# The last 512 columns of v by seven block products, with the mixes' sums by transfer

## The chip, the cores and the metric

The kernel runs on one core of a Trainium2 chip. The time is the device time of one execution in microseconds; before the change it is 993.88 us, the median of three runs (993.27 to 995.94). The core has five engines that run side by side and meet at semaphores: PE (matrix products, with PEld loading its weights), DVE (element by element), ACT (functions and scaled copies), POOL (here fills and the transfers that add), and SP (here transfers alone). Each works its own list in order.

## The reference

Two layers over 512 positions of 1024 channels. The first is a pooling and convolution mixer, the second gated linear attention; each is followed by a gated convolution network. The change lies in the attention's input projection:

```python
q, k, v, r, gl = jnp.split(h, [GLA_DK, 2 * GLA_DK, 2 * GLA_DK + GLA_DV, 2 * GLA_DK + 2 * GLA_DV], axis=-1)
g = jax.nn.log_sigmoid((gl @ w_g2 + b_g).astype(f32)) / GLA_TAU
...
o = o_intra + jnp.einsum('bhnlk,bhnkv->bhnlv', q_in, states)
```

Here `h` is the normed input times `gla_w_in`; q and k have 512 columns, v and r 1024, gl 16. Head h of four uses v's columns 256h to 256h + 255, so v's last 512 columns belong to heads 2 and 3. Inputs and results are float32.

## The kernel before

All activations lie in SBUF with channels on the 128 partitions and 512 positions along the row, as 8 tiles `x`. To keep float32 accuracy, each operand of a product is split in two parts: a high part, a rounding copy on ACT (`hi`, `xh`, `th`), and a low part, what is left, on DVE (`lo`, `xl`, `tl`). A product then takes three passes on PE: high by high, high by low, low by high.

Most projections use seven block products for eight: operands are halved both ways, sums of the quarters are formed, and seven products p1 to p7 of quarter size give the result (`DOWN_SEVEN` is their order). The weights' sums are made on the way in: SP loads a quarter into `s31` (L487), POOL adds two others to it with an accumulating transfer (L491), DVE forms `s2` (L520) and `s4` (L526), and ACT and DVE split the four pieces a1, s31p, s2 and a2 (L509, L515). The sums of x, the *mixes*, come from `mix_parts` (L401 to L437): `ta` and `tb` of each pair of x tiles hold four half-row sums, made on DVE (L413 to L422) from `xg`, a scaled copy by ACT (L406), and then split (L428, L434). p1, p2 and p3 use x's own parts, p5 and p7 use `ta`, p6 and p4 use `tb`.

The attention stage lies between 462.5 and 612 us. First v and gl come by plain products with positions on the partitions: `v_chunk` (L1313 to L1315) in four blocks, of 272 columns (256 of v and 16 of gl) and three of 256, each over eight tiles of x. `v_out` (L1320) copies each result with the scale `y4n` to `vt`, `v_low` (L1330) forms its low part `vl`. Between the chunks stand the sums of squares `ss` (L365), their root y4 on ACT and DVE (L323 to L331), its spread `bc` (L357), the transposes `glT`, and four products z (L1259), the gates' logits, to which DVE adds the bias (L1261). ACT then takes abs, exp and log of each z (L1265, L1269, L1273). After v come four q/k pairs and four r pairs of seven products (L627), with the heads' scores, states and outputs between them.

`run_plan` sets the order: each step is given a planned time by `at`, the steps are sorted by it, and PE, DVE and ACT get their instructions in just that order. SP and POOL are not in the plan's lists; a scheduler places their transfers. Raw weight blocks have three buffers (`raw`), the weight sums of this stage two (`s31`), PSUM eight banks. ACT loads a table of functions when it changes between a root, exp, log and others.

Of the kernel before, what the change touches and what calls it, by code (L numbers as in the profile page):

```python
# [14 lines left out]
P = 128  # L15
# [8 lines left out]
NTT = T // P  # L24
HEADS = 4
EPS = 1e-6
VG = 1040
RANK = 16
STACK = 96
VG_COLS = (272, 256, 256, 256)  # L30
VG_K = ((3, 3, 2), (4, 4), (4, 4), (4, 4))
WBLK = 1024
WPITCH = WBLK + 64
SKEW = 19
# [8 lines left out]
UNIT = 1.364  # L43
MM = 0.2272
PAIR = 7 * UNIT
PLAIN = 8 * UNIT
NORM = 0.46
PE_AT = {"p1": 0, "p2": 1, "p6": 3, "p5": 5, "p7": 6, "p4": 9, "p3": 11}
# [17 lines left out]
VLOW = (1.6, 1.6, 1.6, 1.6)  # L66
ROWS = (1.6, 0.6, 3.6)
SILU = 5.6
ROOT = 2.2
L31 = (-1.4, -1.4)  # L70
KEYS = 1.6
GATE = 3.0
MIXL = 5.8
HALF_AT = ((11.0, 6.6, 5.6), (13.0, 5.2, 4.3))
LEFT_AT = 2.6
EARLY = (0, 2, 4)
# [16 lines left out]


@with_exitstack
def trunk_kernel(ctx, tc, xT, cols, w_first, w_lead, w_ab, w_pool, w_abo, w_vg, w_qk, w_r, w_g2, w_go, w_up, w_dn, w_ds, w_de, out):
    nc = tc.nc
    V, S, G, PE = nc.vector, nc.scalar, nc.gpsimd, nc.tensor

# [8 lines left out]
    def slot(dt=F32, name="s"):  # L108
        return big.tile([P, T], dt, tag="s", name=name)
# [17 lines left out]
    def bank(name="ps"):  # L127
        return ps.tile([P, T], F32, tag="ps", name=name)
# [8 lines left out]
    def col(name, i=0):  # L137
        c = COLS[name] + i
        return colt[:, c : c + 1]
# [56 lines left out]
    def f32(ap):  # L196
        return ap.bitcast(F32)
# [203 lines left out]
    def mix_parts(i, gname, minus_gain):  # L401
        m = {}

        def scale():
            m["x"] = slot(name="xg")
            S.activation(m["x"], x[i], AF.Copy, scale=col(gname, i))  # L406

        def first_sum():
            if "t" in m:
                return  # L410
            xg = m["x"]
            m["t"] = slot(name="ta"), slot(name="tb")
            V.tensor_tensor(m["t"][0][:, lo_t], xg[:, lo_t], xg[:, hi_t], ALU.subtract)  # L413

        def sums():
            xg, x2 = m["x"], x[i + HK]
            first_sum()
            ta, tb = m["t"]
            gain, minus = col(gname, i + HK), minus_gain[:, i : i + 1]
            V.scalar_tensor_tensor(tb[:, lo_t], x2[:, hi_t], gain, ta[:, lo_t], ALU.mult, ALU.add)  # L420
            V.scalar_tensor_tensor(tb[:, hi_t], x2[:, lo_t], minus, tb[:, lo_t], ALU.mult, ALU.add)
            V.scalar_tensor_tensor(ta[:, hi_t], x2[:, hi_t], gain, xg[:, hi_t], ALU.mult, ALU.subtract)  # L422

        def high():
            m["h"] = {}
            for n in (1, 0):
                m["h"][n] = slot(F32R, "th")
                S.activation(m["h"][n], m["t"][n], AF.Copy)  # L428
# [9 lines left out]
        return scale, first_sum, sums, high, low  # L438

    def operands(mixed):  # L440
# [14 lines left out]
    def at(t, fn):  # L455
        events.append((t, len(events), fn))
# [21 lines left out]
        at(t_high, lambda: steps[0]())  # L478
        at(t_low, lambda: steps[1]())

    def seven_weights(src, base, pool, sums, behind=False, lead=None, later=0.0, begin=(26.0, 20.0, 15.4, 9.7), early=0.0, low31=None):
        w = {}

        def load_sum():
# [16 lines left out]
        def tiles(kind, wide):  # L501
            if wide:
                return wsp.tile([P, WPITCH], F32R, tag=kind, name=kind)[:, SKEW : SKEW + WBLK]
            tag, bufs = "s" + kind[0], 2 if pool == "up" else 1
            return stage[pool].tile([P, T + 64], F32R, tag=tag, name=tag, bufs=bufs)[:, SKEW : SKEW + T]

# [32 lines left out]
        when = (-6.75, -4.35, -2.7, -2.4, -1.65, -0.95, -0.3, 1.55, 1.5, 3.3)  # L539
        if pool == "up":  # L540
            when = (*when[:7], *((2.2, 1.5, 4.4) if lead is not None else (0.4, 1.5, 3.3)))
        if pool == "dn":
            when = (-4.2, -2.9, 0.0, -4.0, -2.2, -1.0, -0.3, 4.3, 0.9, 7.2)
        if pool == "gla":
            when = (-6.75, -4.35, -2.1, -1.6, -0.9, -0.2, 0.5, 4.4, 1.5, 5.3)
        if low31 is not None:
            when = (*when[:8], low31, when[9])
        if lead is not None and lead < 2:
# [708 lines left out]
    def gate_logits(h):  # L1257
        zb = bank("z")
        PE.matmul(zb, g2[:, h * P : (h + 1) * P], glT, start=True, stop=True)  # L1259
        heads[h]["z"] = slot(name="z")  # L1260
        V.tensor_scalar(heads[h]["z"], zb, col("b_g", h), None, ALU.add)  # L1261

    def gate_sizes(h):
        e = heads[h]["e"] = slot(name="e")
# [223 lines left out]
        at(t + 0.8, high)  # L1488
        at(t + split, low)

    def mix_in_plan(i, t, last=4.2):
        scale, _, sums, high, low = mix_parts(i, "mix1", minus_gain)

        def done():
            mixed[i] = low()

        at(t, scale)
        at(t + 0.8, sums)
        at(t + 3.0, high)
        at(t + last, done)  # L1500

    t = 0.0

    def then(us, fn):
        nonlocal t
        at(t, fn)
        t += us
# [6 lines left out]
    minus_gain = negated("mix1", 0.0)  # L1514
    mixed = [None] * HK
    for i in range(HK):
        mix_in_plan(i, (7.0, 11.6, 21.0, 25.6)[i], MIXL if i == 2 else 4.2)
    first = True
    for b, (n, ks) in enumerate(zip(VG_COLS, VG_K)):
        k0 = 0  # L1520
# [30 lines left out]
    def pair(src, kind, h, between=None, early=0.0, begin=(26.0, 20.0, 15.4, 9.7), calm=None, low31=None):  # L1551
# [58 lines left out]
        else:  # L1610
# [4 lines left out]
            at(t + soon, lambda: silu(0, left))  # L1615
            at(t + (SILU if h == 1 else soon + 0.7), lambda: silu(1, right))

    def head_keys(h, d=0.0):
        at(t + d, lambda: keys(h))
        at(t + d + 2.4, lambda: keys2(h))  # L1620

    def head_scores(h):
        then(2.1, lambda: scores(h))
        at(t + 0.1, lambda: key_rows(h))
        at(t + 0.1, lambda: masked(h))
        at(t + ROWS[0], lambda: masked_high(h))
        at(t + ROWS[1], lambda: key_lows(h))
        at(t + ROWS[2], lambda: masked_low(h))

    def head_kv(h):  # L1630
        then(1.3, lambda: kv(h))
        at(t + 0.1, lambda: states(h))
# [8 lines left out]
    def gates_of(h, t):  # L1641
        at(t + 2.0, lambda: decays(h))
        at(t + 1.6, lambda: decays2(h))
        at(t + 5.8, lambda: decays3(h))

    def head_gates(h, d, split):
        for e in range(2):
            out_gate(h, e, t + d + 0.75 * e, split)

    gates_of(0, t - 4.0)  # L1650
    pair(w_qk, "qk", 0, calm=0, low31=L31[0])
    head_keys(0, KEYS)
    gates_of(1, t - GATE)
    at(t - 7.5, lambda: log_gate3(3))
    pair(w_qk, "qk", 1, low31=L31[1])
    head_keys(1, 0.2)
    gates_of(2, t - 3.0)
    head_scores(0)
# [211 lines left out]
```

## Time and profile before

| what | value |
|---|---|
| median of three runs | 993.88 us |
| span of the profiled execution | 992.2 us |
| mean granted clock of PE | 0.998 |
| first product of v's block 0 | 462.5 us |
| first product of block 2, first product of q/k pair 0 | 489.0, 511.0 us |

The page gives the profiled execution by its span, from the first to the last instruction; the median of the timed runs is 1.7 us above it, which is what lies around the span and the spread of runs together. In a timeline row stand the start, the time taken, engine, line, operation, output and inputs, shapes, how many such instructions follow each other, and in brackets the idle time ahead with what ended it. An instruction's time overlaps the next one's a little, so a queue's pace is read from start to start.

### The profile page before, as it was taken

Reading aid. Unit: us, or ns where it says so; the run is one execution under the profiler, and the core shown is the slowest. Engines: PE = TensorE matmul, PEld = TensorE weight load, DVE = VectorE, ACT = ScalarE, POOL = GpSimd, SP = SyncE. Lnnn points to the kernel's source line nnn. Section 1 sums busy time; section 2 is a strip of 40 time slices with the busy share of each in tenths; the row PEclk is TensorE's granted clock in tenths of the full one; section 3 lists DMA queues with packets and bytes.
Section 4 is the critical chain, followed back from the end, with each engine's and each line's share of the span. In section 5 each row is a group of like instructions: output and inputs, shape, how many; then the busy total and the mean of one; then the engine's idle time right before and its main releaser. Section 6 shows DMA issues by size and latency. Waiting matters only on the chain.

```text
span 992.2 us, 18669 instructions
## 1 busy us (share of the span) xinstructions
PE 983.8 (99%) x7356; PEld 932.6 (94%) x7356; DVE 891.8 (90%) x1399; ACT 624.7 (63%) x1040; POOL 89.1 (9%) x111
## 2 busy tenths in 40 slices
PE   9999999999999999999999999999999999999997
PEld 7888889999999988999999999899999999988997
DVE  7786689999999999889999889889999999999886
ACT  6432467666667666446776676667766766666553
POOL 0000111101011000002000000111111101000000
PEclk9999999999999999999999999999999999999999
DMA  7423667778877464726426453767788787464622
GB/s 255 130 98 106 167 141 180 192 184 210 202 185 199 103 166 114 189 82 178 123 82 160 108 132 115 193 160 179 205 213 193 191 208 178 120 146 125 168 81 99
DMA packets 69240, 155.22 MB, mean 156 GB/s; under 512 B 5824, under 2 KB 9280, under 8 KB 69152
## 3 DMA queue, kind: packets, MB, share of 16 engines
q1 hardware_dynamic: 50560, 119.03, 37.6%
q0 software_dynamic: 18304, 34.61, 21.3%
q8 instruction: 57, 0.93, 0.4%
q10 hardware_dynamic: 288, 0.40, 0.1%
q14 instruction: 31, 0.25, 0.1%
HBM read 149.29 MB, written 2.10 MB: 153 GB/s over the span
## 4 chain that ended last, share of the span: by engine, by line
PE 90%; DVE 5%; ACT 2%; issue 1%; DMA 1%; DVEq 0%; ACTq 0%
PE stx L627 31%; PE styz L627 17%; PE dn L287 11%; PE go L287 4%; PE abo L287 4%; PE dn L627 3%; PE stz L627 2%; PE pu L1094 2%; PE pc L287 2%; PE pb L287 2%; PE px L287 2%; PE vg L1313 1%; PE vg L1315 1%; PE vg L1314 1%; DMA raw<-in_w_up 1%
## 5 line engine op out<-in xcount | busy, mean ns | idle before, releaser
L515 DVE TENSOR_TENSOR lo<-raw,hi 128x1024 fp32r<-128x1024 f32 x120 | 146.3, 1221 | 3.2 <-ACT hi L509 2.9
L509 ACT ACTIVATE hi<-raw 128x1024 fp32r<-128x1024 f32 x120 | 125.6, 1058 | 35.6 <-PE styz L627 11.2
L491 POOL DMA_DIRECT2D s<-in_w_up x44 | 53.4, 1213 | 477.9 <-ACT yh L200 96.0
L242 ACT ACTIVATE hi<-raw 128x1024 fp32r<-128x1024 f32 (+3 forms) x67 | 59.8, 896 | 26.8 <-PE px L287 9.0
L384 DVE SCALAR_TENSOR_TENSOR cacc<-u,colt,cacc 128x511 f32<-128x511 f32 x96 | 71.6, 746 | 2.6 <-ACT cacc L381 2.5
L246 DVE TENSOR_TENSOR lo<-raw,hi 128x1024 fp32r<-128x1024 f32 (+3 forms) x67 | 68.6, 1028 | 5.3 <-ACT hi L242 4.6
L515 DVE TENSOR_TENSOR lo<-s,hi 128x1024 fp32r<-128x1024 f32 x60 | 73.1, 1218 | 0.0
L381 ACT ACTIVATE cacc<-u,colt 128x512 f32<-128x512 f32 x48 | 39.2, 816 | 43.6 <-DVE u L749 40.0
L627 PE MATMUL stx<-th,hi 128*128 128x256 f32 x416 | 64.6, 277 | 0.8 <-ACT kk L734 0.8
L509 ACT ACTIVATE hi<-s 128x1024 fp32r<-128x1024 f32 x60 | 63.4, 1056 | 2.8 <-issue 1.6
L627 PE MATMUL stx<-th,lo 128*128 128x256 f32 x416 | 64.1, 276 | 0.0
L627 PE MATMUL stx<-tl,hi 128*128 128x256 f32 x416 | 64.1, 276 | 0.0
L627 PE MATMUL styz<-xh,hi 128*128 128x256 f32 x400 | 62.0, 277 | 0.0
L627 PE MATMUL styz<-xh,lo 128*128 128x256 f32 x400 | 61.8, 276 | 0.0
L627 PE MATMUL styz<-xl,hi 128*128 128x256 f32 x400 | 61.6, 276 | 0.0
L627 PEld LDWEIGHTS stx<-th,hi 128*128 128x128 f32 x416 | 54.9, 188 | 1.3 <-ACT kk L734 1.0
L627 PEld LDWEIGHTS stx<-tl,hi 128*128 128x128 f32 x416 | 54.9, 188 | 0.0
L627 PEld LDWEIGHTS stx<-th,lo 128*128 128x128 f32 x416 | 54.9, 188 | 0.0
L627 PEld LDWEIGHTS styz<-xh,hi 128*128 128x128 f32 x400 | 52.9, 188 | 0.1
L627 PEld LDWEIGHTS styz<-xh,lo 128*128 128x128 f32 x400 | 52.8, 188 | 0.0
L509 ACT ACTIVATE sh<-raw 128x512 fp32r<-128x512 f32 x60 | 37.9, 631 | 23.8 <-DVE raw L520 23.7
L627 PEld LDWEIGHTS styz<-xl,hi 128*128 128x128 f32 x400 | 52.8, 188 | 0.0
(416 smaller groups left out, 2704.5 us busy)
## 6 DMA issues: line engine op xcount, KB each, us to landing
s<-in_w_up SPq DMA_DIRECT2D x44, 512.0 KB, 6.7
s<-in_w_up POOLq DMA_DIRECT2D x44, 512.0 KB, 7.2
raw<-in_w_up SPq DMA_DIRECT2D x44, 512.0 KB, 6.4
raw<-in_w_up SPq DMA_DIRECT2D x44, 256.0 KB, 3.2
raw<-in_w_dn SPq DMA_DIRECT2D x32, 320.0 KB, 2.9
raw<-in_w_ab SPq DMA_DIRECT2D x12, 512.0 KB, 3.7
raw<-in_w_abo SPq DMA_DIRECT2D x8, 512.0 KB, 3.5
s<-in_w_ds SPq DMA_DIRECT2D x8, 512.0 KB, 5.8
```

Source lines behind the costliest of these rows:

```text
L242: S.activation(parts[0], raw, AF.Copy)
L246: V.tensor_tensor(parts[1], raw, f32(parts[0]), ALU.subtract)
L287: PE.matmul(out, w[k] if isinstance(w, list) else w[:, k, :], a[k], start=first and i == 0 and k == 0, stop=last and i == 2 and k == n - 1 ...
L381: S.activation(acc[0], u, AF.Identity, bias=col(bname, j), scale=col(wname, 2 * nj + j))
L384: V.scalar_tensor_tensor(a, u[:, : T - i], col(wname, (2 - i) * nj + j), a, ALU.mult, ALU.add)
L491: G.dma_start(w["s31"].rearrange("p (a n) -> p a n", a=2), part, accum_op=ALU.add)
L509: S.activation(h, src(), AF.Copy)
L515: V.tensor_tensor(lo, src(), f32(h), ALU.subtract)
L627: PE.matmul(b[out][:, ts], wt[k], a[k], start=first and i == 0 and k == 0, stop=i == 2 and k == len(a) - 1, skip_group_check=True,)
L1094: PE.matmul(pus[g], parts[k][w][:, g * P : (g + 1) * P], a[k], start=k == 0 and i == 0, stop=k == KD - 1 and i == 2,)
L1313: PE.matmul(o[c][:, :n], xh[kk][:, cs], h[:, k, :], start=kk == 0, stop=False)
L1314: PE.matmul(o[c][:, :n], xl[kk][:, cs], h[:, k, :], start=False, stop=False)
```

## The change

v's first 512 columns (and gl) stay with `v_chunk`, in two blocks. The last 512 are computed by a new `v_pair`, with seven block products, each in two halves of the channels (n = 0 and 1), so there are two sets of seven-weights, loaded from a new array `w_v`. The products' results are copied out of PSUM by ACT (`keep`) and summed by DVE (`add`) as raw rows `vs`, four tiles of 512. Only in the fourth q/k pair are these scaled and split into `vt` and `vl` (`finish`). Since p6, p5 and p7 of `v_pair` need the mixes, these are made earlier, and another way: ACT writes the x part of `tb`, DVE makes the two sums of `ta`, and two accumulating transfers on POOL add `ta` to `tb` and one half of `tb` to the other. The bias of z moves from DVE to ACT. The weight sums of q/k pairs 0 and 1 are loaded later, since `v_pair` takes the two `s31` buffers first.

```diff
-VG_COLS = (272, 256, 256, 256)
+VG_COLS = (272, 256)
+V_WHEN = (
+    (-7.5, -6.0, 1.0, -0.6, 0.2, 1.0, 1.8, 6.0, 3.2, 8.4),
...
+MIX_AT = ((2.0, 17.0), (4.0, 19.0), (6.0, 21.0), (8.0, 24.0))
...
+    def mix_by_dma(i, gname, minus_gain):
+        def scale():
+            m["x"] = slot(name="xg")
+            S.activation(m["x"], x[i], AF.Copy, scale=col(gname, i))
+        def start():
+            tb = slot(name="tb")
+            m["t"] = [slot(name="ta"), tb]
+            S.activation(tb[:, lo_t], x[i + HK][:, hi_t], AF.Copy, scale=col(gname, i + HK))
+            S.activation(tb[:, hi_t], x[i + HK][:, lo_t], AF.Copy, scale=minus_gain[:, i : i + 1])
+        def sums():
+            xg, (ta, tb) = m["x"], m["t"]
+            V.tensor_tensor(ta[:, lo_t], xg[:, lo_t], xg[:, hi_t], ALU.subtract)
+            V.scalar_tensor_tensor(ta[:, hi_t], x[i + HK][:, hi_t], col(gname, i + HK), xg[:, hi_t], ALU.mult, ALU.subtract)
+        def first_add():
+            G.dma_start(tb[:, lo_t], ta[:, lo_t], accum_op=ALU.add)
+        def second_add():
+            G.dma_start(tb[:, hi_t], tb[:, lo_t], accum_op=ALU.add)
...
         heads[h]["z"] = slot(name="z")
-        V.tensor_scalar(heads[h]["z"], zb, col("b_g", h), None, ALU.add)
+        S.activation(heads[h]["z"], zb, AF.Identity, bias=col("b_g", h))
...
+        for wait, step in zip((0.0, 0.7, 0.8, 0.9, 4.5), steps):
+            at(t + wait, step)
+        for n, when in ((0, t + 2.6), (1, late)):
+            at(when, lambda n=n: high(n))
+            at(when + 0.8, lambda n=n: done(n))
...
+    def v_pair():
+            for n in range(2):
+                h, lo = w[n][piece]
+                for c in range(2):
+                    cs = slice(c * P, (c + 1) * P)
+                    for i, (a, wt) in enumerate(((ah, h), (al, h), (ah, lo))):
+                        for k in range(2):
+                            cols = slice(side * QUARTER + k * 256, side * QUARTER + k * 256 + 256)
+                            PE.matmul(b[out][:, c * 256 : c * 256 + 256], a[2 * n + k][:, cs], wt[:, cols],
...
+        def keep(tile, sign):
+            for c in range(2):
+                S.activation(rows_of(tile, c), b["x"][:, c * 256 : c * 256 + 256], AF.Copy, scale=sign)
...
+        for name in DOWN_SEVEN:
+            then(VUNIT, lambda name=name: product(name))
+            ends_at[name] = t
+        at(ends_at["p1"] + 0.1, lambda: keep((0, 0), 1.0))
+        at(ends_at["p6"] + 0.1, lambda: keep((0, 1), 1.0))
...
+        def finish(now):
+            for c in range(NTT):
+                at(now + 1.8 * c, lambda c=c: scaled(c))
+                at(now + 1.8 * c + 0.8, lambda c=c: lows(c))
...
     head_scores(1)
+    finish_v(t + 1.0)
     pair(w_qk, "qk", 3, {3: (lambda: head_kv(1),)}, 4.6)
```

The first place where the order of instructions moves is ACT's list from the logits to the first results. Before, DVE had added the bias, and ACT had the copies of block 1 (`vt`), the abs (`e<-z`) and the first exps (`e<-e`) there, with the splits of a mix between them:

```order
L1320 ACTIVATE vt<-vg_5576,y4n 128x256
L1320 ACTIVATE vt<-vg_5577,y4n 128x256
L1265 ACTIVATE e<-z 128x512
L1320 ACTIVATE vt<-vg_5578,y4n 128x256
L1265 ACTIVATE e<-z 128x512 x2
L1320 ACTIVATE vt<-vg_5579,y4n 128x256
L1265 ACTIVATE e<-z 128x512
L1269 ACT_TABLE_LOAD
L1269 ACTIVATE e<-e 128x512 x2
L428 ACTIVATE th<-tb 128x512
L428 ACTIVATE th<-ta 128x512
L242 ACTIVATE hi<-raw 128x1024
```

After the change, the same stretch of ACT's list, right behind the splits of the mixes' `tb`, begins with the four biases:

```order
L1308 ACTIVATE z<-z,colt 128x512 x4
L1367 ACTIVATE vt<-vg_5612,y4n 128x256
L554 ACTIVATE hi<-raw 128x512
L1367 ACTIVATE vt<-vg_5613,y4n 128x256
L1312 ACTIVATE e<-z 128x512
L1367 ACTIVATE vt<-vg_5614,y4n 128x256
L554 ACTIVATE hi<-s_5466 128x1024
L1312 ACTIVATE e<-z 128x512 x2
L1367 ACTIVATE vt<-vg_5615,y4n 128x256
L1312 ACTIVATE e<-z 128x512
L1316 ACT_TABLE_LOAD
L1316 ACTIVATE e<-e 128x512 x2
```

The four biases, the split of 512 columns (s2 of the first half) and that of 1024 (its s31p) came in; the row that follows is the two copies of p1's result (`vs<-vx`, 128x256 each), which so stand behind the first two exps.

The second place is ACT's list around the root y4 (`y<-ss`). Before:

```order
L325 ACT_TABLE_LOAD
L325 ACTIVATE y<-ss,eps_t 128x4
L428 ACTIVATE th<-tb 128x512
L428 ACTIVATE th<-ta 128x512
L242 ACTIVATE hi<-raw 128x1024
L406 ACTIVATE xg<-xall,colt 128x512
L1530 ACTIVATE rs<-bc 128x512
```

Before these rows stood one `xg`, of mix 0. After the change, the list ahead of the same root, from the second `xg` on:

```order
L451 ACTIVATE xg<-xall,colt 128x512
L474 ACTIVATE th<-ta 128x512
L456 ACTIVATE tb<-xall,colt 128x256
L457 ACTIVATE tb<-xall,minus_gain 128x256
L248 ACTIVATE hi<-raw 128x1024
L451 ACTIVATE xg<-xall,colt 128x512
L474 ACTIVATE th<-ta 128x512
L456 ACTIVATE tb<-xall,colt 128x256
L457 ACTIVATE tb<-xall,minus_gain 128x256
L451 ACTIVATE xg<-xall,colt 128x512
L474 ACTIVATE th<-ta 128x512
L331 ACT_TABLE_LOAD
```

All four `xg`, three pairs of `tb` halves, three splits of `ta` and one weight split now stand ahead of the table load and the root.

The third place is POOL's list in this stage. After the change (the `tb` rows are the mixes' additions; before, the second fill of `att` was followed at once by the weight sums of q/k pair 2):

```order
L534 DMA s_5466<-in_w_v 128x2x512
L534 DMA s_5535<-in_w_v 128x2x512
L1251 MEMSET starts 128x512
L1255 MEMSET maskf 128x512
L1253 MEMSET starts 128x1 x8
L1261 MEMSET att 128x512
L1257 AFFINE_SELECT maskf<-maskf 128x512
L1261 MEMSET att 128x512
L466 DMA tb<-ta 128x256 x2
L470 DMA tb<-tb 128x256 x2
L466 DMA tb<-ta 128x256
L470 DMA tb<-tb 128x256
```

Eight transfers of 128 KB came in, each `tb<-tb` behind a wait for its `tb<-ta`; first and second additions of mixes 2 and 3 alternate.

More of the change, by code (lines that the diff above doesn't have):

```diff
@@ L45 @@
 PAIR = 7 * UNIT
+VUNIT = 2 * UNIT
 PLAIN = 8 * UNIT
@@ L72 @@
 GATE = 3.0
-MIXL = 5.8
 HALF_AT = ((11.0, 6.6, 5.6), (13.0, 5.2, 4.3))
@@ L438, in mix_parts, with high, low @@
         return scale, first_sum, sums, high, low
+    def mix_by_dma(i, gname, minus_gain):
+        m = {}
+        def scale():
[11 more added lines that the diff above has]
+        def first_add():
+            ta, tb = m["t"]
+            G.dma_start(tb[:, lo_t], ta[:, lo_t], accum_op=ALU.add)
+        def second_add():
+            tb = m["t"][1]
+            G.dma_start(tb[:, hi_t], tb[:, lo_t], accum_op=ALU.add)
+        def high(n):
+            m["h", n] = slot(F32R, "th")
+            S.activation(m["h", n], m["t"][n], AF.Copy)
+        def low(n):
+            lo = slot(F32R, "tl")
+            V.tensor_tensor(lo, m["t"][n], f32(m["h", n]), ALU.subtract)
+            return m["h", n], lo
+        return scale, start, sums, first_add, second_add, high, low
     def operands(mixed):
@@ L479, in block, with seven_weights @@
         at(t_low, lambda: steps[1]())
-    def seven_weights(src, base, pool, sums, behind=False, lead=None, later=0.0, begin=(26.0, 20.0, 15.4, 9.7), early=0.0, low31=None):
+    def seven_weights(src, base, pool, sums, behind=False, lead=None, later=0.0, begin=(26.0, 20.0, 15.4, 9.7), early=0.0, low31=None, when=None, shared=None):
         w = {}
@@ L1489, in out_gate, with mix_in_plan, done @@
         at(t + split, low)
[L1491 to L1500, printed above, removed]
+    def mix_in_plan(i, t, late):
+        *steps, high, low = mix_by_dma(i, "mix1", minus_gain)
+        mixed[i] = {}
+        def done(n):
+            mixed[i][n] = low(n)
+        for wait, step in zip((0.0, 0.7, 0.8, 0.9, 4.5), steps):
[3 more added lines that the diff above has]
+            at(when + 0.8, lambda n=n: done(n))
     t = 0.0
@@ L1654, in trunk_kernel @@
     at(t - 7.5, lambda: log_gate3(3))
-    pair(w_qk, "qk", 1, low31=L31[1])
+    pair(w_qk, "qk", 1, begin=(19.0, 14.5, 15.4, 9.7), low31=L31[1])
     head_keys(1, 0.2)
```

74 lines of the change are left out of this document (66 added, 8 removed).

## The prediction

> **The bound.** I read the page's busy times first, then its chain, then the busy times by stretch around the stage that changes (columns: PE, PEld, DVE, ACT, POOL, clock, DMA share, GB/s), and last the timelines.
>
> ```profile
> PE 983.8 (99%) x7356; PEld 932.6 (94%) x7356; DVE 891.8 (90%) x1399; ACT 624.7 (63%) x1040; POOL 89.1 (9%) x111
> PE 90%; DVE 5%; ACT 2%; issue 1%; DMA 1%; DVEq 0%; ACTq 0%
> 480.00:490.00 10.00, 9.81 (x82) 9.29 (x81) 9.83 (x19) 6.60 (x13) 0.00 (x0) 1.00 0.42 121
> 490.00:500.00 10.00, 10.00 (x91) 10.00 (x90) 8.29 (x16) 9.94 (x17) 0.00 (x0) 1.00 0.19 62
> 500.00:510.00 10.00, 10.00 (x91) 10.00 (x90) 9.90 (x15) 7.18 (x11) 0.00 (x0) 1.00 0.17 57
> ```
>
> PE is the bound: 99% busy, 90% of the chain, and here full at a clock of 1.00. So work taken from PE shortens the run, and any new wait of PE lengthens it by its own length. ACT, 63% over the span, is full in 490 to 500, just where the products of v's last columns now run.
>
> **PE's saving.** The rows are PE's, from its timeline (start, length, line).
>
> ```profile
> 475.44 1.05 PE L357 MATMUL bc<-ident,y 128*128 128x128 f32 x8
> 487.69 1.09 PE L1259 MATMUL z<-glT,g2s 96*128 96x512 f32 x4
> 488.97 0.39 PE L1313 MATMUL vg<-hi,xh 128*128 128x256 f32 x1 [0.19 <-DVE z L1261]
> 510.86 0.33 PE L1549 MATMUL stx<-ones 128*128 128x64 f32 x2
> ```
>
> From 488.97 to 510.86 PE runs 192 products of 256 columns for blocks 2 and 3: 21.89 / 192 = 0.114 us each. The seven products have 7 x 24 = 168. -2.7 us, and the 0.19 us wait for DVE's z goes too: -0.2. The rest of PE's order is unchanged. One of the seven (24 matmuls) takes 2.74 us.
>
> **The root.** PE's bc at 475.44 needs y4, the root of the sums. The rows are ACT's timeline, and one of DVE.
>
> ```profile
> 465.76 0.73 ACT L306 ACTIVATE xh<-xall,colt 128x512 fp32r<-128x512 f32 x1 [4.68 <-DVE xall L910]
> 466.91 1.59 ACT L242 ACTIVATE hi<-raw 128x544 fp32r<-128x544 f32 x2
> 469.13 1.28 ACT L325 ACT_TABLE_LOAD   x1
> 472.73 0.26 ACT L325 ACTIVATE y<-ss,eps_t 128x4 f32<-128x4 f32 x1 [2.31 <-DVE v L323]
> 473.42 0.16 DVE L331 SCALAR_TENSOR_TENSOR y<-t,y 128x4 f32<-128x4 f32 x1
> ...
> 487.70 0.71 ACT L406 ACTIVATE xg<-xall,colt 128x512 f32<-128x512 f32 x1
> 488.31 0.81 ACT L1320 ACTIVATE vt<-vg,y4n 128x256 fp32r<-128x256 f32 x2
> 489.03 0.62 ACT L1265 ACTIVATE e<-z 128x512 f32<-128x512 f32 x1
> 489.55 0.47 ACT L1320 ACTIVATE vt<-vg,y4n 128x256 fp32r<-128x256 f32 x1
> 491.96 1.28 ACT L1269 ACT_TABLE_LOAD   x1
> 493.25 1.16 ACT L1269 ACTIVATE e<-e 128x512 f32<-128x512 f32 x2
> 494.31 0.62 ACT L428 ACTIVATE th<-tb 128x512 fp32r<-128x512 f32 x1
> 495.36 1.04 ACT L242 ACTIVATE hi<-raw 128x1024 fp32r<-128x1024 f32 x1
> 496.30 1.14 ACT L1269 ACTIVATE e<-e 128x512 f32<-128x512 f32 x2
> 498.75 2.20 ACT L1273 ACTIVATE e<-e 128x512 f32<-128x512 f32 x4
> 500.86 1.05 ACT L242 ACTIVATE hi<-raw 128x1024 fp32r<-128x1024 f32 x1
> 512.68 0.39 ACT L1571 ACTIVATE q<-stx 128x256 f32<-128x256 f32 x1 [0.47 <-PE stx L627]
> 512.96 0.63 ACT L1298 ACTIVATE bc<-bc 128x512 f32<-128x512 f32 x1
> ```
>
> From start to start ACT takes: xg 0.61, a half with a column scale (vt) 0.36, 512 columns 0.52, 1024 columns 0.94, a table load 1.29, two exps 1.06, four logarithms 2.11, a plain half 0.28. Before, the table load sat idle from 469.13 and y waited for DVE. Now, between the splits that start at 466.91 and y, stand one of 544 (0.55), 4 xg (2.44), 6 halves tb (2.16), 3 splits th (1.56), one of 1024 (0.94) and the load (1.29): 8.9 us, so y starts at 475.8. y4 is done 0.85 later, as before (472.73 to 473.58): 476.7 against 475.44. +1.3 on PE. The tb halves are not in the trace; between the plain half and vt the term is 0.8 to 1.3, and two waits on DVE in between could make it 1.7.
>
> **The mixes.** Eight accumulating transfers of 128 KB go through POOL's queue, behind the two weight sums and the memsets that end near 470.7.
>
> ```profile
> 464.90 2.46 POOL L491 DMA_DIRECT2D s<-in_w_qk  x2 [48.92 <-DMA s<-in_w_qk]
> s<-in_w_qk POOLq DMA_DIRECT2D x2, 512.0 KB, 9.5
> 648.95 0.90 POOL L674 DMA_DIRECT2D acc<-sq  x1 [8.15 <-DMA acc<-sq]
> 653.97 0.86 POOL L674 DMA_DIRECT2D acc<-sq  x1 [3.22 <-DMA acc<-sq]
> DMA to landing us min/median/max: 3.3/5.3/10.5
> ```
>
> The second weight sum is issued near 466.1 and lands 9.5 or more later, so the first mix transfer, queued behind it, lands near 478. Then POOL, in order and 0.87 us a piece, issues second(0), second(1), first(2) at 479.7, waits L for its landing, second(2), first(3), waits L, second(3), waits L: the last lands at 480.6 + 3L. On ACT its split (0.52) and z of head 0 (0.6) follow, and PE's p1 needs that z, whose bank it takes: 481.8 + 3L, against 488.97 + 1.3 = 490.3. The trace has such transfers of 256 KB only, 3.3 to 10.5 us, and POOL restarted 5.0 us after one issued at 648.95. Half the bytes: I bound L by 1.7 (half the shortest) and 5.3 (the median), and take 3.6, nearest the shortest row with some restart. 492.6: +2.3 (0 to 7.4; the wait begins at L = 2.8). Behind that split ACT holds all four z, and DVE behind its low part the first s2 sum, which p6 needs; both lie beside this wait and the next.
>
> [...]
>
> **The stop at p6.** p6 writes the bank of p1, so it waits until ACT has copied p1 out (vs). In ACT's order between z of head 0 and the second vs stand 3 z, 4 vt (1.44), a half-width split (0.52), 4 abs (2.08), one of 1024 (0.94), a load (1.29), 2 exps (1.06), 2 vs (0.56). Scaled z is not in the trace: 0.52 as e, 0.82 as the row of the convolution below, 0.6 taken as xg: 1.8. In all 9.8 us; PE needs 2 x 2.74 = 5.5 for p1 and p2. +4.3 (4.0 to 5.0).
>
> ```profile
> L381 ACT ACTIVATE cacc<-u,colt 128x512 f32<-128x512 f32 x48 | 39.2, 816 | 43.6 <-DVE u L749 40.0
> 516.03 2.36 DVE L515 TENSOR_TENSOR lo<-raw,hi 128x1024 fp32r<-128x1024 f32 x2
> 499.42 0.69 DVE L1277 SCALAR_TENSOR_TENSOR z<-z,e 128x512 f32<-128x512 f32 x1 [1.64 <-ACT e L1273]
> 500.14 1.22 DVE L1279 TENSOR_TENSOR_SCAN bc<-starts,z 128x512 f32<-128x512 f32 x1
> ```
>
> Then 2 exps (1.06), a half split (0.52), a load (1.29), 4 logarithms (2.11), the second half's s31p split (1.05) and behind it its low part on DVE (1.22): 7.3 us, where PE, from p6, comes there after 2.74 + 1.37 + 0.45 = 4.6. +2.8 (2.2 to 3.2).
>
> DVE follows from there: until the second half's low a2, 2 z (0.72 each), 2 scans (1.14) and 2 lows (1.14, 1.22), 6.0 against PE's 5.4: +0.5. Until sh of pair 0, a scan and its z, 8 adds of halves (0.34), a low and two of 512 (0.6), then on ACT sh, two vs and the copy of p1 (1.5): about 7.7 against PE's 6.4 (p4, p1, p2 and a rest), and 0.5 more at its p7: +1.8. Together +2.3 (1.0 to 3.5).
>
> **Fourth pair.** It gains four lows of 512 on DVE and four copies on ACT.
>
> ```profile
> 540.00:550.00 10.00, 10.00 (x85) 9.84 (x84) 9.93 (x21) 6.77 (x18) 1.20 (x1) 1.00 0.65 153
> 556.00 1.08 DVE L1417 SCALAR_TENSOR_TENSOR st<-st,dec,kv 128x256 f32<-128x256 f32 x2 [1.45 <-ACT st L1415]
> 980.00:992.00 12.00, 6.45 (x56) 6.14 (x54) 6.07 (x14) 2.87 (x6) 0.00 (x0) 0.87 0.49 175
> ```
>
> DVE is full up to 550 and has 1.45 idle at 556; 4 x 0.7 = 2.8. +1.1 (0 to 2.8). ACT has room there.
>
> DVE's relief hides nothing: the sums of the mixes (8 halves), four lows, z and eight vl leave it, but two sets of seven-weight splits come in their place. The weight loads keep their places on SP behind the same buffers; their cover is the same stalls.
>
> **Sum** against the profiled span: -2.7 - 0.2 + 1.3 + 2.3 + 4.3 + 2.8 + 2.3 + 1.1 = +11.2, 992.2 to 1003.4. The median of the runs is 1.7 above that span: 1005.1.
>
> **Rivals.**
> - Mixes in time (L up to 2.8): the third term falls, +8.9, 1002.8. For it: only half the bytes, and few other transfers after 480 (DMA share 0.42, 0.19). Against it: the shortest row is 3.3. Chance 0.22. [...]
> - Mixes late (L = 5.3): +16.3, 1010.2. Chance 0.12.
> - The clock falls in PE's new gap of 4 us at p6: for it, the last 12 us, with PE idle for 5.5, show 0.87. That is 12 x 0.13 = 1.6 more, 1006.7. Against: every stretch with short gaps shows 1.00. Chance 0.06. [...]
> - The other side: ACT's list from z to vs ends within p1 and p2. It decides at 5.5 us for 18 instructions; then the terms at p6, p5 and pair 0 fall, and with the mixes in time -2.9 + 1.3 + 1.1 = -0.5, 993.4. Against: each duration above is from a row, and z cannot start before PE's z. Chance 0.07. With y4 and the fourth pair hidden as well, -2.9: 991.0, chance 0.03.
> - That the change does not do what it says is excluded by PE's order: 168 products for 192.
>
> **Numbers.** The forecast, 1005.1, has 0.50. The range takes in mixes in time with every other term at its low end, 1000, and late mixes, 1010, with some of the high ends: 999.5 to 1012.5. A difference of 0.3% (3 us, 990.9 to 996.9) is what a measurement can tell from none: faster 0.02, same 0.08, slower 0.90.
>
> **What would show it.** PE should stop at bc until ACT's y; at p1 for ACT's z, with POOL waiting for its own transfers; at p6 for ACT's vs; in p5 for ACT's hi and DVE's lo. If PE runs through p1 to p4 without a stop and ACT's list is short, I am wrong; if the stop at p1 is long, only L is off.

## The result, and the profile after

The changed kernel takes 1007.09 us, the median of four runs (1006.71 to 1008.92), against 993.58 us before (four runs, 992.86 to 995.94): slower by a ratio of 1.0137, 95% interval 1.0120 to 1.0153. The prediction was 1005.1 with a range of 999.5 to 1012.5. The profiled execution has a span of 1007.2 us. Of all executions reported below one, the profiled one of the run e10_both, ran at a mean clock of 0.65 and took 1413.33 us; it is left out there.

The page after, busy times and chain:

```profile
PE 988.1 (98%) x7332; PEld 934.6 (93%) x7332; DVE 893.6 (89%) x1399; ACT 634.7 (63%) x1060; POOL 97.7 (10%) x121
PE 89%; DVE 4%; ACT 3%; DMA 2%; issue 1%; POOL 0%; DVEq 0%; POOLq 0%; ACTq 0%
```

PE runs 24 instructions less and is busy for 4.3 us longer, 2.7 of them in the stage measured below (146.35 for 143.69). So beside the waits some of its products became slower: at half clock p1's 24 took 5.18 us, as shown below, where 24 at full clock take 2.80. The stretches of the changed kernel (same columns as in the prediction) say where:

```profile
490.00:500.00 10.00, 5.14 (x26) 4.62 (x25) 3.96 (x6) 4.82 (x10) 0.87 (x1) 0.73 0.10 14
500.00:510.00 10.00, 8.41 (x63) 7.92 (x62) 5.90 (x11) 9.94 (x17) 0.99 (x1) 0.93 0.24 79
510.00:520.00 10.00, 8.28 (x67) 7.67 (x66) 7.76 (x10) 8.11 (x14) 1.42 (x2) 1.00 0.75 186
```

Between 490 and 500 every engine is idle for about half of the time or more, and the clock is below 1: all wait for something that is none of them. PE's waits of the changed kernel from 460 to 650 (who, for whom: total us, times, longest):

```profile
PE vx L1702 <- ACT z L1308: 4.9, 1, 4.9
PE bc L363 <- DVE y L337: 1.6, 1, 1.6
PE vx L1702 <- ACT vs L1716: 1.6, 1, 1.6
PE vz L1702 <- ACT hi L554: 1.1, 1, 1.1
PE stx L674 <- ACT q L1620: 0.9, 2, 0.7
PE kv L1448 <- DVE ktl L1442: 0.6, 1, 0.6
PE vz L1702 <- DVE lo L560: 0.5, 1, 0.5
PE stx L674 <- ACT k L1620: 0.4, 1, 0.4
```

These are the stops that were forecast (bc, p1, p6, the high and the low part that p5 needs for its second half, pair 0, and the heads around the fourth pair). Before, PE had one wait of 0.2 us in the same stretch.

The profiles of this study differ by up to 3.5 us in when this stage begins (470.1 to 473.7), with the same products of PE ahead of it. So I measure the **stage** from the first product `ss` to the first product `go`, in each profile. The rows are PE's timeline, two of before and two of the changed kernel:

```profile
471.55 0.95 PE L365 MATMUL ss<-ones,acc 128*128 128x1 f32 x8
615.49 1.53 PE L287 MATMUL go<-yh,hi 128*128 128x512 f32 x6
```

```profile
472.48 0.95 PE L371 MATMUL ss<-ones,acc 128*128 128x1 f32 x8
630.59 1.53 PE L293 MATMUL go<-yh,hi 128*128 128x512 f32 x6
```

143.94 us before, 158.11 after: the stage lost 14.17 us, and 0.93 of the 15.0 us between the spans was there before it began. By the starts of PE's products, the loss falls into the pieces of the table. A stage is read from one execution of each kernel, while the times of one kernel's runs mostly differ by 0.3 (e9_dve_bias) to 4.4 us (e1_warm). A difference of some tenths between two stages therefore shows nothing alone.

| piece of the stage | forecast | measured |
|---|---|---|
| to `bc` (root) | +1.3 | +1.8 |
| to the first product of p1 (z's old wait of 0.2 gone, mixes) | +2.1 | +4.8 |
| p1 to the start of pair 0 (26.80 for 21.89 us) | +4.4 | +4.9 |
| pair 0 | +2.3 | +1.4 |
| from there to `go` | +1.1 | +1.3 |
| sum | +11.2 | +14.2 |

The late start of p1 is POOL's chain. POOL's timeline of the changed kernel:

```profile
471.49 1.80 POOL L466 DMA_DIRECT2D tb<-ta  x2
479.84 0.90 POOL L470 DMA_DIRECT2D tb<-tb  x1 [6.55 <-DMA tb<-ta]
...
481.65 1.16 POOL L466 DMA_DIRECT2D tb<-ta  x1
486.44 0.86 POOL L470 DMA_DIRECT2D tb<-tb  x1 [3.62 <-ACT th L474]
486.98 1.22 POOL L466 DMA_DIRECT2D tb<-ta  x1
492.41 0.87 POOL L470 DMA_DIRECT2D tb<-tb  x1 [4.21 <-issue]
```

POOL issues a first addition, waits for it, issues the second, and again for mix 3. (The releaser named at 486.44 is a guess of the profile: that transfer waits for the first addition to the same `tb`.) From 481.65 the three waits are 4.8, 5.4 and, to the split on ACT at 495.18, 2.8 us. ACT's timeline from there, and last one row of DVE:

```profile
495.18 0.63 ACT L474 ACTIVATE th<-tb 128x512 fp32r<-128x512 f32 x1 [5.31 <-DMA tb<-tb]
495.71 2.41 ACT L1308 ACTIVATE z<-z,colt 128x512 f32<-128x512 f32 x4
505.49 0.64 ACT L1716 ACTIVATE vs<-vx 128x256 f32<-128x256 f32 x2
511.09 1.04 ACT L554 ACTIVATE hi<-s 128x1024 fp32r<-128x1024 f32 x1
512.17 1.23 DVE L560 TENSOR_TENSOR lo<-s,hi 128x1024 fp32r<-128x1024 f32 x1 [2.37 <-ACT hi L554]
```

ACT does not stop again until the split at 511.09; DVE's low part of it ends at 513.40, and p5 goes on at 513.45. From the start of z to there the list takes 17.7 us. And PE, with the granted clock of the first stretches (columns: length, PE busy, PEclk, DMA share, GB/s):

```profile
496.44 0.80 PE L1702 MATMUL vx<-hi,xh 128*128 128x256 f32 x2 [4.86 <-ACT z L1308]
501.62 0.40 PE L1702 MATMUL vy<-hi,xh 128*128 128x256 f32 x2
506.18 0.50 PE L1702 MATMUL vx<-hi,th 128*128 128x256 f32 x2 [1.59 <-ACT vs L1716]
```

```profile
494.00:495.00 1.00, 0.00 (x0) 0.82 0.75 107
495.00:496.40 1.40, 0.00 (x0) 0.50 0.00 0
500.00:501.00 1.00, 1.00 (x7) 0.50 0.00 0
```

The clock went to half while PE stood still, and p1's 24 products took 5.18 us (496.44 to 501.62) where p7 later takes 2.80.

### The profile page after: what moved, and what is told of

Its sections match the earlier page's. It is cut to its first block, busy times and chain, and to the rows that moved or that the text cites. A ratio compares the mean times of both kernels' runs of the same rounds, so it can differ in the third digit from the quotient of the medians.

```text
span 1007.2 us, 18674 instructions
## 1 busy us (share of the span) xinstructions
PE 988.1 (98%) x7332; PEld 934.6 (93%) x7332; DVE 893.6 (89%) x1399; ACT 634.7 (63%) x1060; POOL 97.7 (10%) x121
## 4 chain that ended last, share of the span: by engine, by line
PE 89%; DVE 4%; ACT 3%; DMA 2%; issue 1%; POOL 0%; DVEq 0%; POOLq 0%; ACTq 0%
PE stx L674 33%; PE styz L674 19%; PE dn L293 10%; PE go L293 4%; PE abo L293 4%; PE dn L674 3%; PE pu L1141 2%; PE stz L674 2%; PE pc L293 2%; PE pb L293 2%; PE px L293 2%; DMA tb<-ta 1%; ACT hi L554 1%; PE stw L674 1%; DMA tb<-tb 1%
## 5 line engine op out<-in xcount | busy, mean ns | idle before, releaser
L560 DVE TENSOR_TENSOR lo<-raw,hi 128x1024 fp32r<-128x1024 f32 (+1 forms) x126 | 152.4, 1211 | 8.3 <-ACT hi L554 7.8
L554 ACT ACTIVATE hi<-raw 128x1024 fp32r<-128x1024 f32 (+1 forms) x126 | 131.0, 1051 | 34.1 <-PE styz L674 11.0
L560 DVE TENSOR_TENSOR lo<-s,hi 128x1024 fp32r<-128x1024 f32 x62 | 75.4, 1217 | 2.4 <-ACT hi L554 2.4
L248 ACT ACTIVATE hi<-raw 128x1024 fp32r<-128x1024 f32 (+3 forms) x63 | 55.7, 885 | 29.1 <-PE px L293 9.1
L252 DVE TENSOR_TENSOR lo<-raw,hi 128x1024 fp32r<-128x1024 f32 (+3 forms) x63 | 63.6, 1014 | 8.1 <-ACT hi L248 7.4
L554 ACT ACTIVATE hi<-s 128x1024 fp32r<-128x1024 f32 x62 | 65.5, 1057 | 2.4 <-issue 1.3
```

What stands on the lines that cost most here:

```text
L248: S.activation(parts[0], raw, AF.Copy)
L252: V.tensor_tensor(parts[1], raw, f32(parts[0]), ALU.subtract)
L554: S.activation(h, src(), AF.Copy)
L560: V.tensor_tensor(lo, src(), f32(h), ALU.subtract)
```

## The experiments

Two theories stood against each other. **A**: from the moment that the last addition is split, ACT's list (with DVE's steps between) runs in order to the second half of p5, and sets the time; what PE does or suffers ahead of that, slow clock included, costs nothing. **B**: PE's stop at p1 and the slow clock behind it are lost as such, and each microsecond of them is one of the run. All changes are to the changed kernel or to the experiment named.

**PE kept busy through its stop.**

```diff
         zb = bank("z")
+        for _ in range(20 if h == 3 else 0):
+            PE.matmul(zb, g2[:, h * P : (h + 1) * P], glT, start=True, stop=True)
```

> Only change to the changed kernel: 20 more z products of head 3 (96x512, about 0.22 us each, 4.3 us in all) into head 3's own bank ahead of the real one, so PE works through its stop of 4.9 us at p1. Theory A (ACT's list): from the split of the last mix (495.7) ACT's in-order list of 17.1 us sets when p5 can go on; what PE does ahead of it, a slow clock included, costs nothing. Then the granted clock stays 1.00 from 490 to 502, p1 takes 2.8 us and not 5.2, the stop at p6 grows from 1.6 to about 4.0, p5 goes on at the same moment (513.4), and the time stays at 1007 within 1 us. Theory B (PE's gap and its clock): the slow clock is worth its own 2.4 us, the stop at p6 stays at 1.6, and the time falls to 1004.7.

1006.52 us (1005.75 to 1010.14), the stage 157.19. PE's largest wait, and the last one in v:

```profile
PE vx L1704 <- ACT vs L1718: 3.2, 1, 3.2
...
PE vz L1704 <- DVE lo L560: 0.5, 1, 0.5
```

p1 and p2 ran at full clock (1.00 from 490 to 500), and the wait at p6 doubled. The slow clock did not go, it came behind this wait: 0.50 from 504 to 506, and p6 took 4.47 us. But PE then still waits 0.5 us for DVE's low part in p5, so the list and not the clock sets when p5 goes on. (The additions landed 3.4 us sooner in the stage in this execution; ACT then waited for the real z of head 3, so its list began 0.9 us earlier in the stage, which is the stage's gain.) As A has it.

**The order of POOL's transfers.** `issue_after` puts a transfer behind another one in POOL's list, here the second additions behind the first ones.

```diff
+SECOND_AT = (14.0, 13.0, 11.5, 10.0)
...
-            G.dma_start(tb[:, lo_t], ta[:, lo_t], accum_op=ALU.add)
+            firsts.append(G.dma_start(tb[:, lo_t], ta[:, lo_t], accum_op=ALU.add).ins)
...
-            G.dma_start(tb[:, hi_t], tb[:, lo_t], accum_op=ALU.add)
+            with tc.issue_after(firsts[-1]):
+                G.dma_start(tb[:, hi_t], tb[:, lo_t], accum_op=ALU.add)
...
-        for wait, step in zip((0.0, 0.7, 0.8, 0.9, 4.5), steps):
+        for wait, step in zip((0.0, 0.7, 0.8, 0.9, SECOND_AT[i]), steps):
```

> Only change: the mixes' four first additions are all issued ahead of the four second ones. The last addition should land near 487 and not at 495.1, so the split of mix 3's tb is done ahead of z, and p1's stop falls from 4.9 to about 0.5 us. Theory A (ACT's list): the list now starts with z near 491.4 and not 495.7; p6 stops for about 4 us, p5 goes on near 509.1, and the time falls by about 4.3 us, to 1002.8; if the clock falls in the gap at p6, this costs nothing. Theory B (stop at p1 and slow clock are each worth their length): 4.4 + 2.4 = 6.8 us less, 1000.3.

1002.51 us (1001.95 to 1002.79), the stage 153.76: 4.35 us less (4.6 by the medians of the runs), where A gave 4.3 and B 6.8. POOL's timeline, and PE's largest wait with the last one in v:

```profile
472.82 0.86 POOL L469 DMA_DIRECT2D tb<-ta  x1 [1.68 <-DVE ta L465]
476.79 0.86 POOL L469 DMA_DIRECT2D tb<-ta  x1 [3.11 <-ACT tb L460]
477.54 3.68 POOL L474 DMA_DIRECT2D tb<-tb  x4
```

```profile
PE vx L1706 <- ACT vs L1720: 3.9, 1, 3.9
...
PE vz L1706 <- DVE lo L564: 0.5, 1, 0.5
```

No transfer waits for another one's landing on POOL any more, p1 does not stop, and the stop at p6 is 3.9, close to the 4.3 of the forecast. PE's clock is again at half behind it (0.50 from 501 to 503, p6 takes 4.46 us), and again at no cost, since PE waits for DVE's low part in p5 after it. From the start of z (489.15) to the end of that low part (506.85) the list takes 17.7 us, just as in the changed kernel.

**ACT's list shortened ahead of p6.** On top of that, the gates' functions later:

```diff
-                    at(t + 1.5, lambda h=h: gate_sizes(h))
-                    at(t + 3.4 - 0.1 * h, lambda h=h: log_gate(h))
-                    at(t + 5.8 - 0.1 * h, lambda h=h: log_gate2(h))
+                    at(t + 7.5, lambda h=h: gate_sizes(h))
+                    at(t + 9.4 - 0.1 * h, lambda h=h: log_gate(h))
+                    at(t + 14.8 - 0.1 * h, lambda h=h: log_gate2(h))
...
-                    at(t + 7.2 + 2.2 * h, lambda h=h: log_gate3(h))
+                    at(t + (16.0, 18.2, 20.4)[h], lambda h=h: log_gate3(h))
```

> The order of additions as in the run before, and the gates' abs and exp 6 us later in the plan, their log 9 us later, so that on ACT the copies of p1 (vs) stand behind z, vt and two weight splits, 5.9 us and not 9.8 behind the first z, and the split of s31p of the second half stands 7 us sooner. Theory A: the stops at p6 and in p5 fall to about nothing, and of the 15 us lost there remain the root (1.6), the end of the fourth pair (1.3) and what DVE is late at q/k pair 0 (1 to 2): 996 to 999. Rival: the gates' logs, now about 9 us later, are late for the scans and the decays of head 0, and PE stops in q/k pair 0 or ahead of the first scores instead: 1001 to 1003. Theory B gives the fall of the order alone and 1.6 at p6: about 998.7.

1000.54 us (999.45 to 1003.65), the stage 151.67. The waits at p6 and p5 are gone, as the list theory says, but the rival holds for what they were worth:

```profile
PE stx L678 <- ACT q L1624: 2.2, 1, 2.2
...
PE stx L678 <- DVE sl L564: 1.2, 1, 1.2
...
PE styz L678 <- DVE lo L564: 0.9, 1, 0.9
```

Without the 3.9 + 0.5 us of stops and the slow p6, pair 0 began 7.0 us sooner in the stage than in e2_order; 4.3 us of stops then came in pair 0 and 0.6 more at the heads behind it, so only 2.1 us of the stage were won.

**The mixes by DVE, as before.**

```diff
-        *steps, high, low = mix_by_dma(i, "mix1", minus_gain)
+        scale, _, sums, high, low = mix_parts(i, "mix1", minus_gain)
...
+        at(t, scale)
+        at(t + 0.8, sums)
+        at(t + 3.0, high)
+        at(t + 4.2, done)
```

> Only change: the mixes are made as before the change (one scaled copy on ACT, four half sums on DVE, no transfers), at the planned times of the changed kernel. ACT loses 8 half copies (0.4 us each, six of them ahead of the root), POOL the eight additions, DVE gains 8 half sums (about 0.4 us each, 3.3 us). Theory A: no wait for transfers, so ACT's list starts with z near 491 and p5 goes on near 508; the root comes about 1.6 us sooner: 1001 to 1002. Rival (DVE's relief was worth the transfers): the 3.3 us of sums on DVE make lows late that PE waits for, at p6 and p5, and it stays above 1004.

1007.14 us (1006.06 to 1007.88), the stage 157.04. Neither side had the place right: the wait for transfers is gone, and its room was taken at the root. PE's two largest waits, and two rows of the timeline of all engines:

```profile
PE vx L1700 <- ACT vs L1714: 3.9, 1, 3.9
PE bc L363 <- DVE y L337: 3.7, 1, 3.7
```

```profile
479.04 0.15 DVE L329 TENSOR_SCALAR v<-ss 128x4 f32<-128x4 f32 x1
479.23 0.26 ACT L331 ACTIVATE y<-ss,eps_t 128x4 f32<-128x4 f32 x1 [2.72 <-DVE v L329]
```

DVE's sums and splits of three mixes stand ahead of the small step `v` that the root needs, and ACT waits 2.7 us for it with its table loaded. The clock fell to half behind PE's stop of 3.7 us at bc, too (0.50 from 482 to 484). Against the changed kernel the transfers save nothing that shows, and cost nothing.

**The root ahead of mixes 2 and 3**, on top of the list run (the second additions count from the start of their mix, so these keep about their place):

```diff
-SECOND_AT = (14.0, 13.0, 11.5, 10.0)
-MIX_AT = ((2.0, 17.0), (4.0, 19.0), (6.0, 21.0), (8.0, 24.0))
+SECOND_AT = (14.0, 13.0, 9.0, 8.0)
+MIX_AT = ((2.0, 17.0), (4.0, 19.0), (9.0, 21.0), (10.5, 24.0))
```

> The run e3_order_list and one thing more: mixes 2 and 3 begin at 9.0 and 10.5 us of the plan and not at 6 and 8, so that 2 scaled copies, 2 half copies and one split less (2.5 us) stand ahead of the root on ACT. Theory (the root's 1.6 us at bc are ACT's backlog): the stop at bc falls to 0.2 or less, all that follows moves with it, and the stage is 1.6 us shorter than in e3_order_list: about 999. Rival: the mixes, 2 to 3 us later, now land behind z; then p1 stops for 1 to 2 us and the gain is given back: 1000 to 1001.

1000.39 us (999.27 to 1002.82), the stage 150.80, 0.9 less than e3_order_list; the medians of the runs are 0.15 apart, so that the kernel is faster is not shown. The stop at bc is gone, as expected, and p1 does not stop, but glT now stops for 1.2 us behind `gl` on DVE (the profile names `vl`, which stands right behind it there):

```profile
PE glT L1304 <- DVE vl L1381: 1.2, 1, 1.2
```

**Pair 0's sum, and DVE's order.** The split of the first half's s31p ahead of z and the load of pair 0's sum earlier (`V_WHEN`, entries 3 and 9 of the first row: 1.0 to -1.5 and 3.2 to -0.7; pair 0's `begin` 14, 10 to 17, 12.5).

> As e5_all, and the split of the first half's sum s31p ahead of the four z (it stood behind them on ACT, and its low part behind four vl on DVE), so its buffer comes free about 6 us sooner and the load of q/k pair 0's sum starts as much sooner. Theory (pair 0 stops in e3_order_list, 2.2 and 1.2 us, because its weight sum has to wait for one of two buffers): both stops fall below 0.5 us in all, about 996. Rival (DVE's scans are what is late there): the stops stay, and the time stays near 999.

1000.00 us (999.29 to 1000.29), the stage 150.64: the load's POOL addition was issued 7 us sooner (494.94 for 501.96), and PE's stops in pair 0 were still 2.0 and 1.2 (1.5 and 1.2 in e5_all, with one of 0.9 that went). The sum was not what was late.

On top of that, the scans and `finish` later:

```diff
-        at(t + (16.0, 18.2, 20.4)[h], lambda h=h: log_gate3(h))
-    at(t - 7.5, lambda: log_gate3(3))
-    finish_v(t + 1.0)
+        at(t + (16.0, 25.0, 31.0)[h], lambda h=h: log_gate3(h))
+    at(t + 4.0, lambda: log_gate3(3))
+    finish_v(t + 6.0)
```

> As e6_sum_early, and DVE's work behind v spread: the scans of heads 1 to 3 stand 7 to 20 us later in the plan, and the scaled copies and low parts of v's last columns begin 5 us later, in and behind the fourth pair. Theory (what is left in pair 0 and at heads 1 and 2, about 2 us, is DVE's backlog of 520 to 560): about 1.5 us less than e6_sum_early, 994 to 995, no longer clearly slower than before, and 168 products for 192 then just pay for themselves. Rival: the backlog is only moved, and PE stops at a later head instead: the same as e6_sum_early.

1005.92 us (1003.82 to 1007.90), the stage 156.16: worse by 5.5. Pair 0 ran with stops of 2.0 and 0.2, and then PE stopped for 3.6 us for a low part behind the scans that had been put later, and for 1.8 at the key lows behind the later `finish`. DVE is busy for 92 to 99% of each 10 us from 520 to 560, and what is put off there stands in front of something else.

On top of e6_sum_early instead, three lists in another order:

```diff
+TA_AT = (2.6, 2.6, 5.0, 5.0)
...
-        for n, when in ((0, t + 2.6), (1, late)):
+        for n, when in ((0, t + TA_AT[i]), (1, late)):
...
-    at(12.5, lambda: V.tensor_copy(mask, maskf))
+    at(20.5, lambda: V.tensor_copy(mask, maskf))
...
-                    at(t + (16.0, 18.2, 20.4)[h], lambda h=h: log_gate3(h))
+                    at(t + (16.0, 20.6, 21.0)[h], lambda h=h: log_gate3(h))
...
-    gates_of(0, t - 4.0)
+    gates_of(0, t - 4.0, 5.7)
```

> As e6_sum_early, and three moves: the splits of the ta of mixes 2 and 3 and the mask's cast stand behind gl on DVE (glT stopped for 1.2 us there), the exp of head 0's decays with its table load stands behind the copy of q on ACT (1.95 us at the first sh product of pair 0), and the scan of head 1 behind the sums of pair 0 on DVE (1.2 us there). Theory (these stops are lists in order, each as long as what stands ahead): the three stops fall below 1 us together and the slow clock behind them goes, 4 to 6 us less than e6_sum_early: 994.5 to 996. Rival (ACT and DVE have too much work between z and pair 1, whatever the order): the stops come back at the decays of head 0, at pair 1 or ahead of the first scores, and it stays above 998.

998.73 us (six runs of 998.07 to 999.67, one of 1007.36), the stage 149.87, and its variant e12_early, with pair 0's weights 2 us earlier in the plan:

> As e8_order_all, with pair 0's weight loads, sums and splits 2 us earlier in the plan, so that on DVE its s2 sum stands ahead of the scan of head 0 and its s4 sum ahead of the scan of head 1, where ACT stood idle for 1.35 us for it (PE stops there: 1.24 and 2.29 us). Theory (pair 0 is late by the order on DVE alone): the first of these stops goes and the second falls to about 1, 2 to 3 us less than e8_order_all: 996. Rival (there is more work on ACT and DVE between z and pair 1 than PE's time there, so any order only moves the stop): the sum of PE's stops from p1 to the first scores stays within 0.7 us of the 3.5 there, about 998.5.

999.29 us (996.95 to 1000.19), the stage 149.32. In both the rival holds: the stop at the first `sh` product of pair 0 goes or shrinks, and one of 2.3 us stands at a later product of pair 0, each time with a slow clock behind it: 0.50 from 519.5 to 521 in e8_order_all, and in e12_early four products take 0.85 us there (519.13 to 519.98) for 0.45 later (523.11 to 523.56). PE's rows of e8_order_all:

```profile
512.71 0.73 PE L679 MATMUL stx<-th,sh 128*128 128x256 f32 x4 [1.24 <-ACT q L1625]
518.00 0.74 PE L679 MATMUL stx<-th,hi 128*128 128x256 f32 x4 [2.29 <-ACT q L1625]
```

These are the fastest that I found: 1.0059 (1.0036 to 1.0083) and 1.0047 (1.0029 to 1.0064) of the kernel before. None beats it.

**The bias of z on DVE**, as before, in the changed kernel and in e8_order_all:

```diff
-        S.activation(heads[h]["z"], zb, AF.Identity, bias=col("b_g", h))
+        V.tensor_scalar(heads[h]["z"], zb, col("b_g", h), None, ALU.add)
```

> Only change to the changed kernel: the bias of z goes back to DVE (four of 0.7 us there, 2.4 us off ACT's list). Head 0's bias then stands on DVE ahead of the low part of mix 3, so p1 waits neither for the additions nor for ACT. Theory A (ACT's list from the split of the last mix on): p1 runs near 491.9 at full clock, its stop of 4.9 and the 2.4 of slow clock are gone, but ACT begins its list at the same moment and has 2.4 us less in it, so the stop at p6 grows to 5 or more and the time falls by 2.4 us alone: 1004.5. Theory B (PE's stop at p1 and the clock behind it are what is lost): at least 4.9 us less, 1002 or lower.

1006.39 us (1006.17 to 1006.50), the stage 157.91. PE's stops:

```profile
490.79 0.50 PE L1702 MATMUL vx<-hi,xh 128*128 128x256 f32 x2 [1.10 <-DVE z L1308]
495.24 0.50 PE L1702 MATMUL vy<-hi,xh 128*128 128x256 f32 x2 [1.37 <-DVE z L1308]
503.67 0.80 PE L1702 MATMUL vx<-hi,th 128*128 128x256 f32 x2 [5.36 <-ACT vs L1716]
```

This speaks against B: p1 ran ahead of the last addition (split at 493.17), p2 behind it, both at full clock (1.00 from 490 to 500), and the stage is only 0.2 us shorter; all went into the stop at p6 and the slow clock there (0.50 from 503.6 to 507). A's 2.4 us did not come either. ACT, with four instructions less, then stood 1.7 us for the s2 sum, which on DVE stands behind the low part of mix 3 and a bias:

```profile
495.88 0.63 ACT L554 ACTIVATE hi<-raw 128x512 fp32r<-128x512 f32 x1 [1.71 <-DVE raw L565]
```

So the list that counts is that of ACT and DVE together, from the last addition on.

> As e8_order_all with the bias of z on DVE. Theory: DVE sits idle for 1.5 us around z and ACT is full from there to pair 0, so 2.4 us off ACT's list are worth 0 to 1 us more than e8_order_all, 994 to 996. Rival: DVE's 2.8 us delay the first s2 sum, and p6 stops for 1 to 2 us: 997.

1000.60 us (four runs, 999.92 to 1001.73), not less than e8_order_all. There is no profile at full clock, so why stays open.

**The end of the fourth pair.** This run leaves out the low parts of v's last columns (zeros in their place).

```diff
-            V.scalar_tensor_tensor(vlows(c, T, T), raw[c], y4n[:, c : c + 1], f32(vcols(c, T, T)), ALU.mult, ALU.subtract)
+            G.memset(f32(vlows(c, T, T)), 0.0)
```

> The changed kernel without the low parts of v's last 512 columns: in place of DVE's four subtractions in and behind the fourth q/k pair (4 x 0.74 us), POOL fills these four tiles with zeros, so the products that take them add nothing. Theory (the 1.3 us lost between the second q/k pair and the last product of the stage are DVE's four extra subtractions): PE's stops at the copy of k (0.43) and at the key lows (0.60) go, and the time falls by 1.0 to 1.3 us. Rival (the order of the steps there, or ACT's four scaled copies, makes these stops): they stay as they are, and the time falls by less than 0.3 us.

1006.36 us (1005.79 to 1006.78), the stage 156.99. From the first product of the stage to the copy of k in the fourth pair it is 0.5 us shorter, before anything that was left out, and another 0.6 us from there to its end. The stop at the key lows (0.60) is gone, the one at the copy of k (0.43) stays: half of what is lost there is DVE's four subtractions, the rest is not.

## Why the prediction was right

The time lies 2.0 us above the forecast, inside its range, and PE stopped at the places that were named. By the terms of the sum:

- **PE's saving.** 2.7 was forecast. At full clock a product of 24 takes 2.80 (p7), so seven take 19.6 for 21.89: 2.3.
- **The root.** Forecast +1.3, the wait is 1.6. That ACT's backlog ahead of the root makes it was shown by moving mixes 2 and 3 behind it (the wait at bc went).
- **The mixes.** The mechanism was right, POOL in order and each second addition behind its first one's landing, and removing the alternation removed the stop. The term mis-sized is L. From the issue of mix 2's first addition at 481.65 to the last landing are 13.5 us; less 0.9 for that issue these are the forecast's 3 L, so L was 4.2 for 3.6, inside the bounds of 1.7 and 5.3. That is 1.8 us, and the issue itself stood 1.0 later in the stage than forecast (480.7 with the 0.9 us taken off that the stage began later, for 479.7). Together this is nearly all of the 3 us by which the stage was longer than forecast. In another execution with the same transfers (e1_warm) they landed 3.4 us sooner in the stage, with an L of 3.4, so L was not the same in two executions. In the changed kernel the second additions landed in 2.7 to 3.0 us, the first ones, issued behind others, in 4.2 to 8.4, so the rival with its L of up to 2.8 did not come.
- **The stops at p6 and in p5.** From the start of z to the end of DVE's low part, 495.71 to 513.40, less head 0's z (0.6), are 17.1 us, the forecast's 9.8 + 7.3. (Its terms for p6 add up to 9.7 and not 9.8, and 7.3 less 4.6 is 2.7 and not 2.8, so the agreement is to 0.2.) Their division was wrong, 1.6 at p6 for 4.3 and 1.6 in p5 for 2.8. What failed there is the step "PE needs 2 x 2.74 = 5.5 for p1 and p2": at half clock p1 alone took 5.2. In e2_order, where p1 ran at full clock (2.9 us, 489.89 to 492.81), p6 stopped for 3.9.
- **The rival of the clock**, given 0.06, did come, though at p1 and not at p6. Its price was wrong: 1.6 was to be added, and it cost nothing, since PE was ahead of ACT anyway. Two runs that kept the clock up at p1 (e1_warm, e9_dve_bias) did not get faster for it (1006.52 and 1006.39 us for 1007.09); there it was at 0.50 in p6, and PE still had to wait 0.5 us in p5.
- **A premise that failed**: "any new wait of PE lengthens it by its own length". In e9_dve_bias the stop of 4.9 us at p1 became 1.1, and 1.4 at p2, the slow clock there went, and the stage was only 0.2 us shorter. The sum came out all the same, because its terms at p6 and in p5 were counted as one list from z on.
- **Pair 0 and the fourth pair.** Forecast 2.3 and 1.1, measured 1.4 and 1.3. That DVE's backlog makes the latter holds for half of it.
- **The other side**, ACT's list within p1 and p2, asked for 5.5 us of list. Where the list was cut to about that (e3_order_list), the stops went to pair 0, and all reordering together won 8.8 of 14.2 us of the stage. What is left is 5.4 us more than before (149.32 for 143.94 in e12_early). DVE and ACT gained two sets of seven-weight splits and the copies and sums of the results, and gave up less: in the stage ACT is busy 112.0 us in the changed kernel for 103.0 before, DVE 134.2 for 131.8. That this work, and not an order that nobody tried, keeps the stage from the time before is argued, not shown.

## What to carry to other kernels

A change that takes work from the bound engine pays only if what it gives to the others fits beside what is left: count their lists in order, from the event that starts them to the instruction that the bound engine needs, and compare with its time over the same stretch. A stop ahead of the end of such a list was not worth its own length here: with the stop at p1 down from 4.9 us to 1.1, 1.4 more at p2 and the slow clock gone from p1, the stop at p6 grew from 1.6 to 5.4 us, the slow clock came there, and the stage was 0.2 us shorter (e9_dve_bias). To test this, look whether the engine still waits at the list's end. An engine that issues chained transfers in order should issue all the first ones before it waits for any; here this was worth 4.4 us of the stage.

## What was not expected of the hardware

The clock's fall stood at no fixed distance from PE's stop in these profiles, and it lasted beyond the restart. In the changed kernel PE stopped near 491.6, and the clock was at 0.50 from about 494.6 to 501.5, some 5 us of it with PE at work. The fall came 3.1 us after the stop began there, 2.2 in e9_dve_bias, and 3.9, just behind the restart, in e2_order. Shorter stops were followed by it, too. In e8_order_all, stops of 1.24 and 2.29 us with 3.0 us of work between them were followed by half clock, 1.4 us after PE had gone on (columns as above):

```profile
515.50:518.00 2.50, 0.21 (x3) 1.00 0.30 105
518.00:519.50 1.50, 1.50 (x12) 0.97 0.62 61
519.50:521.00 1.50, 1.50 (x9) 0.50 0.98 173
```

In e12_early a single stop of 2.30 us there was followed by it (mean clock 0.92 from 510 to 520 and 0.91 from 520 to 530), and in e7_spread one of 1.84 us at the key lows (0.97 from 560 to 580, 0.94 from 580 to 600); in e3_order_list, stops of 2.20 and 1.18 us in pair 0 left the clock at 1.00. How long it stayed at half is worked out from the mean clocks of the stretches. It is about 3.4 us in eleven falls of eight of these profiles (3.40 to 3.43 in the five that short stretches show: e1_warm, e2_order, e6_sum_early, e8_order_all and the one at bc in e4_dve_mix). In the changed kernel and in e9_dve_bias, where PE stood for 1.8 and 3.2 us of that time, it is 6.8. Why the clock falls, and why it stays for as long, no run here shows.
